# A two-layer decoder on one core: most large products by Strassen's seven products, x spilled between the norms, score operands padded to 128 rows

## The chip, the cores and the metric

One core of a Trainium2 chip runs the whole program. The metric is device time in microseconds (us) of one execution, the median over runs. Engines are named as in the profile: PE (TensorE, the matrix engine), DVE (VectorE), ACT (ScalarE), POOL (GpSimd), SP (SyncE, which here only issues DMAs).

## The reference

The input x is 512 tokens by 1024 features. Each of two layers is a half-step SwiGLU FFN ("A"), a mixing part ("M") and a second FFN ("B"); every part is wrapped in two RMS norms:

```python
for l in range(DEPTH):
    x = x + 0.5 * rms_norm(swiglu(rms_norm(x, g[0]), w_ffn1_in[l], w_ffn1_out[l]), g[1])
    y = mixing_sublayer(rms_norm(x, g[2]), mem, ...)
    x = x + rms_norm(y, g[3])
    x = x + 0.5 * rms_norm(swiglu(rms_norm(x, g[4]), w_ffn2_in[l], w_ffn2_out[l]), g[5])
```

`swiglu` multiplies by 1024 x 5632 weights, forms silu(a) * b (2816 wide), and multiplies back to 1024. The mixing part projects h to z (2048 wide: queries, keys and values), runs three attentions on it (16 heads: 6 of a sliding window with sinks, 6 dilated in three groups, 4 into 256 memory tokens), multiplies three branch projections by sigmoid gates (h times 1024 x 3072 weights), adds them and projects once more (`w_o`). All data are float32.

## The kernel before

All data lie transposed: features on the 128 partitions, tokens along the row, so that x is eight tiles (`X`) of 128 x 512, resident in SBUF throughout. To keep float32 accuracy at the matrix engine's float32r rate, each operand is split into a high part (a rounding copy on ACT) and a low part (the difference, on DVE), and a product is three matmuls, hi\*hi, hi\*lo and lo\*hi (`mm3`, line 348). Weights come as 128 x 1024 blocks of 512 KB: `load` (line 308) issues the DMA on SP into a `raw` tile, ACT writes `wh`, DVE writes `wl` = raw - wh. Five slots each hold raw, wh and wl tiles.

A product of a 128 x 128 weight block and 512 tokens is one matmul of 512 columns (`group`, line 361). Only the first unit of each stage (tiles ab0, z0, and the last four tiles of a stage's output, y_A, y_B, y_wM) goes in two halves of 256 tokens, so that it can begin while the other half's norm is not finished. Per FFN, `ffn` (line 471) runs 11 units of a (two 128-feature tiles), b (two) over k = 8: 96 matmuls of 512 columns each, or 192 of 256 for the first. The output goes in three chunks of 8, 8 and 6 of the 22 middle tiles, with PSUM results added to Y on DVE: 456 matmuls of 512 and 144 of 256. In the mixing part, z takes 192 matmuls of 256 and 288 of 512, the gates 576 of 512.

The norm's scale R is not applied to h: the product runs on x * gain, and DVE multiplies each result by R when it takes it out of PSUM (POOL does so once more for the FFN's b half, behind the silu, line 490) (ab -> s, line 488; z, line 637; gates, line 901). So the matrix engine can begin a stage before R is known. `tail` (line 444) ends each stage: half i's sum of squares, `rstd_cols` (PE column sums, DVE, POOL's power), `rows` (PE spreads the result over the partitions), `post_tile` (x += y * R * gain), `pre_tile` (the next h in two parts), and `pre_stat` for the next R.

In the attentions, `stack_q` (line 709) puts a head's high part on its 64 partitions and its low part on the other 64, `stack_k` (line 720) the high part of the key twice. A score block is then one matmul over 128 rows and one more over 64 rows with the key's low part (`scores`, line 733). Softmax: DVE takes the maximum, ACT the exponentials, POOL divides (`norm_p`), PE transposes, and `pv` (line 762) multiplies by the values, 64 output rows at a time, first all blocks of head g = 0, later all of g = 1. Sigmoids run behind the last exponential (`nc.behind(last_exp)`, line 903).

The order is not the program's. The class `Plan` records all operations with a rank (program order, weights 250 ranks ahead), and `Plan.run` (line 155) replays them with assumed costs: each engine takes, of the operations whose inputs and slots are there, the one of lowest rank. The result is a fixed instruction order for each engine, and semaphores keep the dependences. As all instructions are emitted in one place, every record of the trace has line 250; tiles are told apart by their names.

Of the kernel before, what the change touches and what calls it, by code (L numbers as in the profile page):

```python
# [14 lines left out]
P = 128  # L15
# [5 lines left out]
N_BIG, N_RAW, N_WH, N_WL = 51, 5, 5, 5  # L21
AHEAD = 250
NEG = -1e30
CHUNKS = ((0, 8), (8, 8), (16, 6))
# [7 lines left out]
class Plan:  # L32
    """Records the program in order and emits it as a list schedule: each engine takes, of the operations
    whose operands and tile slots are there, the one of the lowest rank."""
# [10 lines left out]
    class _Pool:  # L45
        def __init__(self, plan, pool, bufs, reserve):
            self.plan, self.pool, self.bufs, self.reserve = plan, pool, bufs, reserve

        def tile(self, shape, dtype, name, tag="t", bufs=None):
            kw = {} if bufs is None else {"bufs": bufs}  # L50
            t = self.pool.tile(shape, dtype, tag=tag, name=name, **kw)
            self.plan.home[t.tensor.name] = (self.pool.name if hasattr(self.pool, "name") else id(self.pool), tag)
            self.plan.slots[self.plan.home[t.tensor.name]] = bufs or self.bufs
            self.plan.reserve[self.plan.home[t.tensor.name]] = self.reserve
            return t

    def __init__(self, tc, ctx):
        self.tc, self.ctx = tc, ctx
        self.ops, self.hist = [], {}
        self.home, self.slots, self.reserve = {}, {}, {}  # L60
        self.rank, self.also = 0, set()
# [3 lines left out]
    def pool(self, name, bufs, space=None, reserve=None):  # L65
        """reserve: slots that only the tile next in rank may take; None: tiles come in rank order."""
        kw = {"space": space} if space is not None else {}
        return Plan._Pool(self, self.ctx.enter_context(self.tc.tile_pool(name=name, bufs=bufs, **kw)), bufs, reserve)
# [8 lines left out]
    @contextmanager  # L77
    def behind(self, ops):
        """What is recorded here also waits for these operations."""
# [51 lines left out]
    def _cost(self, engine, op, outs, ins, k):  # L131
        """The schedule's weights: how long the engine is held, and when the result is there."""
# [6 lines left out]
        if engine == "tensor":  # L139
            n = self._width(outs[0])  # L140
            t = max(n / 2.4, 54) * (4 if op == "matmul" and ins[0].dtype == F32 and n > 1 else 1)
            return t, t + 220
        psum = any(v.space == PSUM for v in outs + ins)
        if engine == "scalar":
            t = 100 + 0.833 * n + 93 * sum(is_ for is_ in (hasattr(k.get("scale"), "ap"), hasattr(k.get("bias"), "ap"),
                                                         k.get("accum_out") is not None))
        elif engine == "vector":
            slow = {"tensor_copy": 1.04 if psum else 0.52, "tensor_scalar": 1.04 if psum else 0.52, "memset": 0.3,
                    "reciprocal": 8.4}
            t = 70 + slow.get(op, 1.04) * n  # L150
        else:
            t = 630 if k.get("op") == ALU.pow else 100 + {"tensor_tensor": 2.2, "tensor_copy": 3.4}.get(op, 0.91) * n
        return t, t + 200

    def run(self):
# [4 lines left out]
        uses, first = {}, {}  # L160
        for i, (_, _, _, _, _, preds, tiles, rank) in enumerate(ops):
# [3 lines left out]
            for t in tiles:  # L165
                uses[t] = uses.get(t, 0) + 1
                first.setdefault(t, (rank, i))
        queue = {}
        for t, r in sorted(first.items(), key=lambda x: x[1]):
            queue.setdefault(self.home[t], []).append(t)  # L170
# [8 lines left out]
        def fits(i):  # L179
# [4 lines left out]
            for h, ts in need.items():  # L184
                if free[h] < len(ts):
                    return False
                front = queue[h][head[h]] in ts
                r = self.reserve[h]
                if not front and (r is None or free[h] - len(ts) < r):
# [6 lines left out]
        while len(order) < n:  # L196
            moved = False
            for e in self.ENGINES:
# [20 lines left out]
                for t in ops[got][6]:  # L219
                    if t not in placed:  # L220
                        placed.add(t)
                        h = self.home[t]
                        free[h] -= 1
                        while head[h] < len(queue[h]) and queue[h][head[h]] in placed:
# [29 lines left out]
def trunk(ctx, tc, xT, memT, rel, gains, mgains, sinks, bgate, w1i, w1o, wz, wkv, wg, wbr, wo, w2i, w2o,  # L254
# [3 lines left out]
    const = pool("const", 1, reserve=0)  # L258
    xpool = pool("xpool", 1, reserve=0)
# [785 lines left out]
```

## Time and profile before

| | |
|---|---|
| median of 3 runs | 2342.35 us (2339.41 to 2342.63) |
| the profiled execution: span of its instructions | 2345.8 us |
| PE busy | 2308.3 us, 98% of the span |
| DVE, ACT, POOL busy | 1070.0, 862.3, 422.1 us (46, 37, 18%) |
| DMA | 216 MB, 92 GB/s on average |

The profiled execution's own time is not listed apart from its span, which lies 3.4 us above the median of the runs. In a timeline row, the first number is the start in us from the span's start, the second the duration; a matmul's recorded duration includes its way through the array, so the pace of a stream of matmuls is read from starts, not from durations.

### The profile page before, as it was taken

Reading aid. Unit: us, or ns where it says so; the run is one execution under the profiler, and the core shown is the slowest. Engines: PE = TensorE matmul, PEld = TensorE weight load, DVE = VectorE, ACT = ScalarE, POOL = GpSimd, SP = SyncE. Lnnn points to the kernel's source line nnn. Section 1 sums busy time; section 2 is a strip of 40 time slices with the busy share of each in tenths; the row PEclk is TensorE's granted clock in tenths of the full one; section 3 lists DMA queues with packets and bytes.
Section 4 is the critical chain, followed back from the end, with each engine's and each line's share of the span. In section 5 each row is a group of like instructions: output and inputs, shape, how many; then the busy total and the mean of one; then the engine's idle time right before and its main releaser. Section 6 shows DMA issues by size and latency. Waiting matters only on the chain. (4 is left out here: it accounts for less than half of the span.)

```text
span 2345.8 us, 29066 instructions
## 1 busy us (share of the span) xinstructions
PE 2308.3 (98%) x11496; PEld 1929.2 (82%) x11496; DVE 1070.0 (46%) x1713; ACT 862.3 (37%) x1477; POOL 422.1 (18%) x450
## 2 busy tenths in 40 slices
PE   8999999999999999999999999999999999999997
PEld 7788889777888888888888888897778889888886
DVE  5424346644544552443473343475445436424343
ACT  5323234554333532322343232255453335332231
POOL 5401013210112320101231100141101214101012
PEclk9999999999999999999999999999999999999998
DMA  6433333112223222332233333321112322323231
GB/s 206 125 99 110 119 99 100 64 37 63 81 90 100 81 100 81 108 102 96 81 99 99 98 110 120 99 89 56 52 39 91 100 80 92 107 91 107 72 108 37
DMA packets 67080, 216.22 MB, mean 92 GB/s; under 512 B 8010, under 2 KB 15231, under 8 KB 66944
## 3 DMA queue, kind: packets, MB, share of 16 engines
q1 hardware_dynamic: 65344, 211.64, 28.1%
q0 software_dynamic: 1600, 2.72, 0.5%
q8 instruction: 90, 1.47, 0.2%
q14 instruction: 46, 0.38, 0.0%
HBM read 210.91 MB, written 3.42 MB: 91 GB/s over the span
## 5 line engine op out<-in xcount | busy, mean ns | idle before, releaser
L250 POOL TENSOR_TENSOR s<-s,R_wM 128x512 f32<-128x512 f32 (+1 forms) x48 | 69.4, 1449 | 534.2 <-ACT s L250 534.2
L250 ACT ACTIVATE s<-s 128x512 f32<-128x512 f32 (+1 forms) x96 | 56.2, 593 | 214.2 <-DVE s L250 214.2
L250 POOL TENSOR_TENSOR s<-s,R_B 128x512 f32<-128x512 f32 (+1 forms) x24 | 32.3, 1350 | 271.7 <-ACT s L250 261.4
L250 POOL TENSOR_TENSOR s<-s,R_s 128x512 f32<-128x512 f32 (+1 forms) x24 | 31.9, 1333 | 242.2 <-ACT s L250 231.8
L250 DVE TENSOR_TENSOR x<-x,upd 128x256 f32<-128x256 f32 x88 | 44.5, 533 | 0.0
L250 POOL TENSOR_TENSOR g02M<-g02M,g00M 128x512 f32<-128x512 f32 x2 | 2.6, 1282 | 209.5 <-issue 209.5
L250 POOL TENSOR_TENSOR sq_A<-sq_A,sq_A 128x256 f32<-128x256 f32 x24 | 19.8, 843 | 49.0 <-ACT sq_A L250 43.0
L250 POOL TENSOR_TENSOR sq_B<-sq_B,sq_B 128x256 f32<-128x256 f32 x24 | 18.3, 783 | 56.1 <-ACT sq_B L250 55.9
L250 DVE TENSOR_TENSOR wl_a4B<-raw_a4B,wh_a4B 128x1024 fp32r<-128x1024 f32 x4 | 4.9, 1226 | 41.3 <-ACT wh_a4B L250 41.3
L250 DVE TENSOR_TENSOR wl_a4A<-raw_a4A,wh_a4A 128x1024 fp32r<-128x1024 f32 x4 | 4.9, 1225 | 41.3 <-ACT wh_a4A L250 41.3
L250 ACT ACTIVATE hh_wM<-x,gt 128x256 fp32r<-128x256 f32 x32 | 15.2, 505 | 21.0 <-DVE x L250 20.9
L250 DVE TENSOR_TENSOR wl_wo1M<-raw_wo1M,wh_wo1M 128x1024 fp32r<-128x1024 f32 x8 | 9.9, 1257 | 27.8 <-ACT wh_wo1M L250 27.6
L250 DVE SCALAR_TENSOR_TENSOR hl_A<-x,gt,hh_A 128x256 fp32r<-128x256 f32 x32 | 21.8, 699 | 0.0
L250 DVE TENSOR_TENSOR wl_o01A<-raw_o01A,wh_o01A 128x1024 fp32r<-128x1024 f32 x8 | 9.8, 1226 | 24.4 <-ACT wh_o01A L250 24.2
L250 DVE TENSOR_TENSOR wl_o01B<-raw_o01B,wh_o01B 128x1024 fp32r<-128x1024 f32 x8 | 9.8, 1225 | 24.4 <-ACT wh_o01B L250 24.1
L250 DVE TENSOR_TENSOR wl_o11B<-raw_o11B,wh_o11B 128x1024 fp32r<-128x1024 f32 x8 | 9.8, 1225 | 24.4 <-ACT wh_o11B L250 24.1
L250 DVE TENSOR_TENSOR wl_o11A<-raw_o11A,wh_o11A 128x1024 fp32r<-128x1024 f32 x8 | 9.8, 1225 | 23.2 <-ACT wh_o11A L250 22.9
L250 PE MATMUL ab0B<-hh_wM,wl_b0B 128*128 128x256 f32 x64 | 18.3, 286 | 1.7 <-DVE wl_b0B L250 1.7
L250 ACT ACTIVATE hh_A<-x,gt 128x256 fp32r<-128x256 f32 x32 | 15.2, 504 | 12.4 <-DVE x L250 12.3
L250 ACT CAST wh_a8A<-raw_a8A 128x1024 fp32r<-128x1024 f32 x4 | 4.2, 1054 | 41.9 <-PE y11A L250 33.2
L250 ACT CAST wh_a8B<-raw_a8B 128x1024 fp32r<-128x1024 f32 x4 | 4.2, 1054 | 41.9 <-PE y11B L250 33.2
L250 POOL TENSOR_TENSOR sq_q0A<-sq_q0A,sq_q0A 128x256 f32<-128x256 f32 x14 | 17.3, 1236 | 11.7 <-ACT sq_q0A L250 8.1
(2804 smaller groups left out, 8158.9 us busy)
## 6 DMA issues: line engine op xcount, KB each, us to landing
raw_o00A<-in_w1o SPq DMA_DIRECT2D x8, 512.0 KB, 3.4
raw_o01A<-in_w1o SPq DMA_DIRECT2D x8, 512.0 KB, 3.4
raw_o10A<-in_w1o SPq DMA_DIRECT2D x8, 512.0 KB, 3.4
raw_o11A<-in_w1o SPq DMA_DIRECT2D x8, 512.0 KB, 3.5
raw_wo0M<-in_wo SPq DMA_DIRECT2D x8, 512.0 KB, 3.9
raw_wo1M<-in_wo SPq DMA_DIRECT2D x8, 512.0 KB, 3.9
raw_o00B<-in_w2o SPq DMA_DIRECT2D x8, 512.0 KB, 3.3
raw_o01B<-in_w2o SPq DMA_DIRECT2D x8, 512.0 KB, 3.4
```

The source lines that it names most:

```text
L250: getattr(getattr(self.tc.nc, e), op)(*a, **k)
```

## The change

- **Seven products.** The product of weights in 2 x 2 blocks (two output tiles i by two halves of the features j) and activations in 2 x 2 blocks (halves of the features, halves of the tokens) is formed with seven block products instead of eight, in Strassen's form by Winograd: four sums of weight blocks (s1 to s4, POOL), four of activation blocks (t1 to t4, POOL), and seven additions of results (ACT copies, DVE). Each of the seven weight operands is split into high and low parts. All matmuls have 256 columns. It is used for units 2 to 10 of each FFN's input product (`gated`, `quarters`), all of the output product (`out_chunk`, `out_last`, chunks of 2, 3, 3 and 3 of the 11 pairs of middle tiles), the gates (six blocks of `quarters`), and units 2 and 3 of four of z. Units 0 and 1 of the FFN and of z stay direct, in halves of 256 tokens (`direct`, 192 matmuls of 256 each).
- **Norms.** h is now multiplied by R before it is split (`Hs.half`), because t1 to t4 add tokens of different R. So R of a half must be known before the first matmul on that half, and `next_h` runs: update of x, sum of squares, R, h, for one half and then the other. The results no longer need a multiplication by R.
- **x spilled.** x is written to DRAM by SP when h is formed (`spill`, four DMAs of 256 KB a half) and read back before the next update (`load_x`); there are 63 big tiles in place of 51.
- **Attention.** The key's low part is padded with zeros to 128 rows, so both score matmuls have 128 rows. `pv` takes the heads g = 0 and 1 of each block in turn. The factor 1/8 of the queries moves into `stack_q`.
- **Others.** The memory's keys and values are computed inside `next_h`, between the two halves, before the mixing part. The bias tables' 39 DMAs go to SP's queue instead of POOL's. The sigmoid of a block's first quarter reads PSUM directly. `Plan` has new cost figures and another rule for slots; weights have 7 raw, 4 wh and 4 wl slots.

The core of the diff:

```diff
-N_BIG, N_RAW, N_WH, N_WL = 51, 5, 5, 5
-AHEAD = 250
+N_BIG, N_RAW, N_WH, N_WL = 63, 7, 4, 4
...
-CHUNKS = ((0, 8), (8, 8), (16, 6))
+CHUNKS = ((0, 2), (2, 3), (5, 3), (8, 3))
...
+    def parts2(r, n, nm):
+        h = whp.tile([P, 1024], F32R, tag="wh", name="wh_" + nm)
+        lo = wlp.tile([P, 1024], F32R, tag="wl", name="wl_" + nm)
+        nc.scalar.copy(h[:, :n], r[:, :n])
+        nc.vector.tensor_tensor(lo[:, :n], r[:, :n], h[:, :n].bitcast(F32), op=ALU.subtract)
+        return h, lo
...
+        def sum(self, a, b, op, nm):
+            n = self.c * 256
+            s = raw.tile([P, 1024], F32, tag="raw", name=f"{nm}_{self.nm}")
+            nc.gpsimd.tensor_tensor(s[:, :n], a[:, :n], b[:, :n], op=op)
+            return s
...
+        b11, b12, b21, b22 = u0[:, :HF], u0[:, HF:], u1[:, :HF], u1[:, HF:]
+        ta = big.tile([P, S], F32, tag="b", name="ta_" + nm)
+        tb = big.tile([P, S], F32, tag="b", name="tb_" + nm)
+        t1, t3, t2, t4 = ta[:, :HF], ta[:, HF:], tb[:, :HF], tb[:, HF:]
+        nc.gpsimd.tensor_tensor(t1, b12, b11, op=ALU.subtract)
+        nc.gpsimd.tensor_tensor(t2, b22, t1, op=ALU.subtract)
+        nc.gpsimd.tensor_tensor(t3, b22, b12, op=ALU.subtract)
+        nc.gpsimd.tensor_tensor(t4, b21, t2, op=ALU.subtract)
...
+            two(u0[:, :HF], ["b11"], HF)
+            two(u1, ["b21", "b22"], S)
+        two(ta, ["t1", "t3"], S)
+        two(tb, ["t2", "t4"], S)
+        return f
...
+    def product(bk, w, pairs, key, first):
+        for p, f in enumerate(pairs):
+            for b in range(2):
+                dst = bk[:, b * HF:(b + 1) * HF]
+                wh, wl = at(w, p, b)
+                xh, xl = f[key]
+                end = p == len(pairs) - 1 and b == 1
+                nc.tensor.matmul(dst, wh, xh, start=first and p == 0 and b == 0, stop=False, skip_group_check=not first)
+                nc.tensor.matmul(dst, wh, xl, start=False, stop=False, skip_group_check=not first)
+                nc.tensor.matmul(dst, wl, xh, start=False, stop=end, skip_group_check=not first)
...
+        with nc.ahead(-AHEAD):
+            a11 = blk.raw(0, 0)
+            w1 = blk.parts(a11, "a11")
+            s3 = blk.sum(a11, blk.raw(1, 0), ALU.subtract, "s3")
+            w7 = blk.parts(s3, "s3")
+            s1 = blk.sum(blk.raw(1, 0), blk.raw(1, 1), ALU.add, "s1")
+            w5 = blk.parts(s1, "s1")
+            s2 = blk.sum(s1, a11, ALU.subtract, "s2")
+            w6 = blk.parts(s2, "s2")
+            w2 = blk.parts(blk.raw(0, 1), "a12")
+            w4 = blk.parts(blk.raw(1, 1), "a22")
+            s4 = blk.sum(blk.raw(0, 1), s2, ALU.subtract, "s4")
+            w3 = blk.parts(s4, "s4")
+        A, D = bank(mmp, "A" + nm), bank(mmp, "D" + nm)
+        C, B = bank(mmp, "C" + nm), bank(mmp, "B" + nm)
+        e = big.tile([P, S], F32, tag="b", name="e" + nm)
+        fg = big.tile([P, S], F32, tag="b", name="fg" + nm)
+        product(A, w1, pairs, "b11", True)
+        nc.scalar.copy(e, A)
+        product(D, w7, pairs, "t3", True)
+        nc.scalar.copy(fg, D)
+        product(C, w5, pairs, "t1", True)
+        nc.vector.tensor_tensor(fg, fg, C, op=ALU.add)
+        product(B, w6, pairs, "t2", True)
+        nc.vector.tensor_tensor(e, e, B, op=ALU.add)
+        product(A, w2, pairs, "b21", False)
+        c11(A)
+        others(1, 1, fg, e)
+        product(D, w4, pairs, "t4", False)
+        others(1, 0, e, D)
+        product(C, w3, pairs, "b22", False)
+        others(0, 1, e, C)
...
+    def spill(half, nm):
+        for m in range(4):
+            t = dram.tile([P, S], F32, tag=f"xs{half}{m}{nm}", name=f"xs{half}{m}{nm}")
+            nc.sync.dma_start(t, X[half][m])
+            spilled[half][m] = (t, False)
...
+        def half(self, half, R, l, n):
+            for m in range(4):
+                key = m // 2, half, m % 2
+                nm = f"{m}{half}{self.nm}"
+                u = self.u[key] = big.tile([P, S], F32, tag="b", name="hn" + nm)
+                hi = self.hi[key] = big.tile([P, S], F32R, tag="b", name="hh" + nm)
+                lo = self.lo[key] = big.tile([P, S], F32R, tag="b", name="hl" + nm)
+                for b in range(2):
+                    c = slice(b * HF, b * HF + HF)
+                    f = m // 2 * 4 + 2 * b + m % 2
+                    nc.vector.scalar_tensor_tensor(u[:, c], X[half][m][:, c], gcol(l, n, f), R[:, :HF], op0=ALU.mult, op1=ALU.mult)
+                nc.scalar.copy(hi, u)
+                nc.vector.tensor_tensor(lo, u, hi.bitcast(F32), op=ALU.subtract)
...
+    def next_h(l, n, nm, update, blk, first=None, filler=None):
+        h = Hs(nm)
+        for half in range(2):
+            if update is not None:
+                update(half)
+            h.half(half, stat(X[half], f"q{half}{nm}", op), l, n)
+            if update is not None:
+                spill(half, nm)
+            if half == 0:
+                if filler is not None:
+                    h.extra = filler()
+                h.w = (first or direct_weights)(blk)
+        h.finish()
...
+            def others(i, half, x, y):
+                t = x if (i, half) == (1, 1) else big.tile([P, S], F32, tag="b", name="c")
+                nc.vector.tensor_tensor(t, x, y, op=ALU.add)
+                nc.scalar.activation(t[:, :HF], t[:, :HF], AF.Silu)
+                nc.vector.tensor_tensor(u[i][:, HALVES[half]], t[:, :HF], t[:, HF:], op=ALU.mult)
+            quarters(blk, h.pairs, f"{g}{nm}", c11, others)
+            return u
...
+        def out_chunk(ci, pairs):
+            c0, cn = CHUNKS[ci]
+            first = ci == 0
+            for s in range(2):
+                blk = Block(wout[l, s], c0, cn, f"o{ci}{s}{nm}")
+                with nc.ahead(-AHEAD):
+                    w = weights(blk, ("a11", "s3", "s1", "s2", "a12", "a22", "s4"), {})
+                A, D, C, B = (bank(mmp, f"{x}{ci}{s}{nm}") for x in "ADCB")
+                product(A, w["a11"], pairs, "b11", True)
+                take(s, "E", A, first)
+                product(D, w["s3"], pairs, "t3", True)
+                take(s, "F", D, first)
...
+                product(C, w["s4"], pairs, "b22", False)
+                take(s, "C", C, first)
...
-            nc.gpsimd.dma_start(vec[h0:h0 + nh, :n], v[:nh, :n])
+            nc.sync.dma_start(vec[h0:h0 + nh, :n], v[:nh, :n])
...
+                lo = t[:, n:] if 2 * n <= S else big.tile([P, S], F32R, tag="b", name=f"kl{g}{name}")
+                nc.vector.memset(lo[b, :n].bitcast(F32), 0.0)
                 nc.vector.tensor_tensor(lo[a, :n], z[a], t[a, :n].bitcast(F32), op=ALU.subtract)
...
         def scores(dst, qs, ks, g, qcols, kcols):
-            a, _ = parts(g)
             hi, lo = ks
             nc.tensor.matmul(dst, qs[g][:, qcols], hi[g][:, kcols], start=True, stop=False)
-            nc.tensor.matmul(dst, qs[g][a, qcols], lo[a, kcols], start=False, stop=True)
+            nc.tensor.matmul(dst, qs[g][:, qcols], lo[g][:, kcols], start=False, stop=True)
...
                 for j, kb in enumerate(ks):
-                    lhs = V[:, kb * P + vcol:kb * P + vcol + 64] if kind != "mem" else V[:, kb, vcol:vcol + 64]
-                    nc.tensor.matmul(o[64 * g:64 * g + 64, cols(b)], lhs, T[i], start=(j == 0),
-                                     stop=(j == len(ks) - 1))
+                    for g in range(2):
+                        c = vcols[g]
+                        lhs = V[:, kb * P + c:kb * P + c + 64] if kind != "mem" else V[:, kb, c:c + 64]
+                        nc.tensor.matmul(o[64 * g:64 * g + 64, cols(b)], lhs, Ts[g][i], start=(j == 0),
+                                         stop=(j == len(ks) - 1))
...
+            def c11(A):
+                for b in range(2):
+                    sigmoid(b, 0, tile_of(b, 0)[:, :HF], A[:, b * HF:(b + 1) * HF])
```

In `out_last` the products that make the first half of the tokens come first for both halves of the output features, and the two products with s1 and s4, which only the second half needs, come last. The second half of `w_o` runs its two halves of the tokens one after the other in the same way, 96 matmuls of 256 each.

## Rows read from the trace of the kernel before

**Rows 1.** The page: busy time of each engine, granted clock in 40 slices

```profile
PE 2308.3 (98%) x11496; PEld 1929.2 (82%) x11496; DVE 1070.0 (46%) x1713; ACT 862.3 (37%) x1477; POOL 422.1 (18%) x450
...
PEclk9999999999999999999999999999999999999998
```

**Rows 2.** Busy time by stretch (us, engine busy (x count), clock, DMA): seams, start, end

```profile
0.00:40.00 40.00, 30.54 (x215) 28.95 (x216) 24.96 (x43) 26.74 (x59) 24.24 (x35) 1.00 0.78 250
370.00:430.00 60.00, 56.91 (x466) 55.91 (x465) 45.81 (x88) 32.36 (x69) 28.25 (x30) 1.00 0.27 89
760.00:835.00 75.00, 72.44 (x511) 67.10 (x510) 41.31 (x73) 38.56 (x79) 31.48 (x33) 1.00 0.27 85
1150.00:1210.00 60.00, 57.36 (x422) 54.12 (x422) 45.20 (x85) 29.86 (x66) 30.31 (x35) 1.00 0.25 80
...
2315.00:2346.00 31.00, 17.20 (x134) 16.65 (x132) 13.92 (x35) 2.92 (x7) 13.27 (x18) 0.78 0.20 69
```

**Rows 3.** Timeline of PE: first and last of 28 successive 512-wide products

```profile
299.74 0.39 PE L250 MATMUL ab8A<-hh_s,wl_b8A 128*128 128x512 f32 x1
...
305.86 0.39 PE L250 MATMUL ab8A<-hh_s,wl_b8A 128*128 128x512 f32 x1
```

**Rows 4.** Timeline of PE: first and last of 30 successive 256-wide products

```profile
32.01 0.28 PE L250 MATMUL ab0A<-hh_s,wh_b0A 128*128 128x256 f32 x1
...
35.48 0.28 PE L250 MATMUL ab0A<-hh_s,wl_a0A 128*128 128x256 f32 x1
```

**Rows 5.** Timeline of PE: score matmuls of 256, then of 128 columns

```profile
432.51 0.38 PE L250 MATMUL s0m00M<-k0c0M,q0c0M 128*128 128x256 f32 x1
432.82 0.38 PE L250 MATMUL s0m00M<-klc0M,q0c0M 64*128 64x256 f32 x1
...
558.26 0.32 PE L250 MATMUL sob10M<-klb1M,q0b1M 64*128 64x128 f32 x1
558.51 0.33 PE L250 MATMUL sob10M<-k0b1M,q0b1M 128*128 128x128 f32 x1
```

**Rows 6.** Timeline of PE: probabilities times values, and the product behind

```profile
509.20 1.09 PE L250 MATMUL oa1M<-pta11M,VvaM 128*64 128x128 f32 x8
510.22 0.50 PE L250 MATMUL z4M<-hh_A,wl_z4M 128*128 128x512 f32 x1
```

**Rows 7.** Timelines of DVE and POOL: both busy at once, or one alone

```profile
169.15 1.23 DVE L250 TENSOR_TENSOR wl_b5A<-raw_b5A,wh_b5A 128x1024 fp32r<-128x1024 f32 x1 [0.21 <-ACT wh_b5A L250]
...
169.73 1.80 POOL L250 TENSOR_TENSOR s<-s,R_s 128x512 f32<-128x512 f32 x1 [4.18 <-ACT s L250]
...
622.90 1.29 POOL L250 TENSOR_TENSOR g02M<-g02M,g01M 128x512 f32<-128x512 f32 x1 [0.76 <-DVE g01M L250]
...
29.52 0.74 POOL L250 TENSOR_TENSOR sq_s<-sq_s,sq_s 128x256 f32<-128x256 f32 x1
30.91 4.11 POOL L250 TENSOR_TENSOR sq_s<-sq_s,sq_s 128x256 f32<-128x256 f32 x3
...
30.93 1.81 DVE L250 TENSOR_TENSOR wl_a1A<-raw_a1A,wh_a1A 128x1024 fp32r<-128x1024 f32 x1 [1.50 <-ACT wh_a1A L250]
```

**Rows 8.** Timelines around one norm: sum, root, row, update

```profile
380.00 0.50 PE L250 MATMUL st_p0A<-ones,sq_A 128*128 128x1 f32 x4
...
382.64 0.48 DVE L250 SCALAR_TENSOR_TENSOR upd<-y0A,gt,row_p0A 128x256 f32<-128x256 f32 x1 [1.45 <-PE row_p0A L250]
383.04 0.47 DVE L250 SCALAR_TENSOR_TENSOR upd<-y1A,gt,row_p0A 128x256 f32<-128x256 f32 x1
383.43 0.41 DVE L250 TENSOR_TENSOR y5A<-y5A,y_A 128x256 f32<-128x256 f32 x1
...
386.16 2.00 ACT L250 CAST wh_vc<-raw_vc 128x1024 fp32r<-128x1024 f32 x2 [0.42 <-ACT sq_q0A L250]
```

**Rows 9.** Busy time from the last z product to the last Exp; that Exp

```profile
550.00:598.00 48.00, 48.00 (x239) 36.11 (x238) 18.88 (x92) 24.19 (x72) 0.00 (x0) 0.93 0.14 45
...
597.32 0.22 ACT L250 ACTIVATE wgtM<-wgtM 128x24 f32<-128x24 f32 x1 [2.76 <-DVE wgtM L250]
```

More of the change, by code (lines that the diff above doesn't have):

```diff
@@ L166, in run @@
                 uses[t] = uses.get(t, 0) + 1
-                first.setdefault(t, (rank, i))
-        queue = {}
+                first[t] = min(first.get(t, (rank, i)), (rank, i))
+                last[t] = max(last.get(t, (rank, i)), (rank, i))
+        queue, place = {}, {}
         for t, r in sorted(first.items(), key=lambda x: x[1]):
-            queue.setdefault(self.home[t], []).append(t)
+            q = queue.setdefault(self.home[t], [])
+            place[t] = len(q)
+            q.append(t)
+        left = {}
+        for h, q in queue.items():
+            live, room = [], []
+            for t in q:
+                while live and live[0] < first[t]:
+                    heapq.heappop(live)
+                heapq.heappush(live, last[t])
+                room.append(self.slots[h] - len(live))
+            if min(room) < 0 and not self.turns[h]:
+                raise RuntimeError(f"{h}: {-min(room)} slots short, first at {next(t for t, r in zip(q, room) if r < 0)}")
+            left[h] = room
         head = {h: 0 for h in queue}
@@ L186, in fits @@
                     return False
-                front = queue[h][head[h]] in ts
-                r = self.reserve[h]
-                if not front and (r is None or free[h] - len(ts) < r):
+                far = max(place[t] for t in ts)
+                if far - head[h] >= len(ts) and self.turns[h]:
+                    return False
+                if far - head[h] >= len(ts) and min(left[h][head[h]:far], default=len(ts)) < len(ts):
                     return False
@@ L223, in run @@
                         free[h] -= 1
+                        for at in range(head[h], place[t]):
+                            left[h][at] -= 1
                         while head[h] < len(queue[h]) and queue[h][head[h]] in placed:
@@ new lines, in direct @@
+    def direct(h, w, nm, evict):
+        for t, tok in enumerate(HALVES):
+            banks = [bank(mmp, f"{nm}{t}{b}") for b in range(2)]
+            for k in range(KD):
+                for b in range(2):
+                    for i in range(2):
+                        wh, wl = at(w[i, k // 4], k % 4, b)
+                        xh, xl = h.parts(k, t)
+                        dst = banks[b][:, i * HF:(i + 1) * HF]
+                        nc.tensor.matmul(dst, wh, xh, start=k == 0 and i == 0, stop=False)
+                        nc.tensor.matmul(dst, wh, xl, start=False, stop=False)
+                        nc.tensor.matmul(dst, wl, xh, start=False, stop=k == KD - 1 and i == 1)
+            evict(t, banks)
@@ L647, in z_group, with z_at @@
[L647 to L653 removed]
+        def z_at(nme, half):
+            rate = {"qb1": 4, "kb1": 4, "vb1": 4, "qb2": 16, "kb2": 16, "vb2": 16}.get(nme, 1)
+            if nme not in Z:
+                Z[nme] = big.tile([P, S], F32, tag="b", name=f"{nme}{nm}")
+            if rate == 1:
+                return Z[nme][:, HALVES[half]], lambda v: v
+            n = HF // rate
+            return (Z[nme].rearrange("p (r i) -> p r i", r=rate)[:, :, half * n:(half + 1) * n],
+                    lambda v: v.rearrange("p (i r) -> p r i", r=rate))
```

649 lines of the change are left out of this document (382 added, 267 removed).

## The prediction

> **What bounds the kernel now.** I read the page first: PE is busy 98% of the span, and its clock is full but for the end [rows 1]. Such a share says only that something is always in the array, so the pace comes from starts in PE's timeline: 28 products of 512 columns start 6.12 us apart from first to last, 0.2267 us each [rows 3]; 30 of 256 columns 3.47 us, 0.1197 us each [rows 4]. A 256-column product costs 53% of a 512-column one, so each cut in two adds 0.0127 us. Next the busy time by stretch: where one part hands over to the next, PE idles 3.1, 2.6 and 2.6 us (60 less 56.91, 75 less 72.44, 60 less 57.36); the start costs 9.5 and the end 13.8 us [rows 2]. So the kernel is bound by the number of matmul columns, and the sum starts there. DVE (46%) and POOL (18%) look free, but the change loads both.
>
> **Matmuls removed.** Per FFN, before: 240.7 us in (192 x 0.1197 + 960 x 0.2267) and 120.6 us out (456 x 0.2267 + 144 x 0.1197), together 361.3 [rows 3, 4]. After, at the same pace: two direct units of 192 and nine units of 7 x 24 = 168, and an output of 11 x 84 = 924, all of 256: 46.0 + 181.0 + 110.6 = 337.6 us. An eighth of the columns goes, but half of that is given back, since all products are of 256. Four FFNs: -95 us if PE stays the bound. Gates: 576 x 0.2267 = 130.6 us become 1008 x 0.1197 = 120.7 per layer, -20 us in all. z: 88.3 become 86.2, -4 us. The Trainium skill (TensorE: Matmul & The Clock Gate, Wait — 56ns, not 53.3ns?) puts the fixed cost of a product at about 2.5 ns beyond columns over 2.4 GHz; the rows give 13, five times that. By the page the cut in two would cost almost nothing, and the removal would come to about 60 us more; the rows decide.
>
> **What feeds the matmuls.** One unit of seven products lasts 168 x 0.1197 = 20.1 us on PE. For it DVE must do work with two operands in SBUF: seven wl of 1024 elements (1.23 us [rows 7]), four of 512 (0.68, between 0.41 at 256 and 1.23 at 1024 [rows 7, 8]) and four of 256 (0.41): 13.0 us; successive instructions overlap by 0.08 us (0.48 long, 0.40 apart [rows 8]), so 11.8 us. POOL adds four weight sums of 1024 (0.74 at 256 and 1.29 at 512 give 2.4 [rows 7]) and four of 256: 12.5 us. Alone, each fits in 20.1 us. Together they don't: while DVE's wl_b5A ran (169.15 to 170.38), POOL's 512-wide product took 1.80 instead of 1.29 us, ending 1.15 us behind DVE's end; and wl_a1A, begun with POOL at work, took 1.81 instead of 1.23 [rows 7]. They take turns. So a unit needs about 24.3 us of the shared path against 20.1 on PE and 21.8 before (96 x 0.2267). An output block of three pairs needs DVE 6.2 and POOL 7.4 us, 13.6 of PE's 126 x 0.1197 = 15.1 (its additions read PSUM, and I count them free of this). A chunk of three units and two output blocks: 72.9 + 27.2 = 100.1 us in turns, 90.5 on PE. A handover to POOL saves 0.14 us (1.29 less 1.15), one back to DVE as much, of which 0.08 is counted; if they alternate at all of POOL's 32 instructions, 100.1 comes down to about 94. I take the middle, 97. The first chunk (two direct units, two pairs: 46.0 + 20.1 us) stays PE's. An FFN is then 66.1 + 3 x 97 = 357 us, -4, and -15 us for four, where PE alone would give -95. Bounds: 90.5 a chunk (-95), and 117 if DVE's PSUM work (2.8 us a unit, 8.6 in two output blocks) never runs beside POOL's (+220). Gates need 18 to 19 us in turns of PE's 20.1, with the merges' additions between: I take -15 of the -20.
>
> **Scores.** Score matmuls alternate between 128 and 64 rows, and start 0.31 us apart at 256 columns, 0.25 at 128 [rows 5], where same-shape products take 0.12 [rows 4]: a switch of row shape costs 0.19. Per layer 80 of 256 and 48 of 128: two layers 160 x 0.31 + 96 x 0.25 = 74 us; without the switch 160 x 0.12 + 96 x 0.06 = 25. I take -48.
>
> **Values.** The 208 products of probabilities and values run as two records of 0.109 us each, 45 us (8 records in 0.87 us and an exit of 0.2 [rows 6]). In turns between the two column halves they may overlap (-22) or pay that exit, some 0.09, each time (+19). The nearest row is the same-shape stream itself, which gives 0, and half as many entries and exits; I take -10.
>
> **Attention's stalls.** From the last z product to the last Exp, 48 us, PE was 100% busy, but it filled the time with gates [rows 9]. Now a gate block's first quarter stays in its bank until that Exp, so PE has one block (20 us) and most of a second as filler, and its own attention work shrinks by 12 to 17 us. If the chain of DVE and ACT keeps its 48 us, PE lacks 0 to 15 us a layer. POOL's sums also queue ahead of `norm_p`. I take +8 a layer, +16.
>
> **Seams.** h now waits for R. From a half's last result: addition 0.7, square 0.6, addition 0.7, and from st to the update 2.64 [rows 8]; update of four tiles 4 x (2 x 0.40 + 0.6) = 5.6; square and sum 1.5; R again 2.64; the first tile of h two multiplications, an ACT copy and a difference, 2.2: some 17 to 18 us to the first matmul. Under it PE has 72 products (8.6 us) behind an FFN and 96 (11.5) behind `w_o`; before the mixing part also the memory's 96 (11.5). The second half's chain shares DVE with the first's, and ends some 2 us behind the 11.5 us of matmuls of the first. So PE idles 8.5 us at M to B (twice) and 11 at B to A (once), 2 at A to M (twice), and after the long gaps its clock falls once each, 3.4 us (48 us at 0.93 [rows 9]). Against [rows 2] that is +9 (two times), +12 and -1 (two times). At the start, the first matmul waits for x, R and h, to about 17 us where it was 7, partly won back in the streams: +6. The end's chain is about 2 us shorter. Sum +32; bounds +10 and +70. The cover here is short: anything late in this chain is late on PE.
>
> **SP.** Each half's four spills and loads of x (256 KB) and the 39 table DMAs stand in SP's one queue, and a spill that waits for DVE's x holds the weight loads behind it. Weights are loaded four products ahead, which hides it; if not, one or two landings are exposed, 0 to +7. I take +2. Landings themselves have room at the share of [rows 2].
>
> **Sum.** FFN -15, gates -15, z -4, scores -48, values -10, attention +16, seams +32, SP +2: -42 us. The profiled execution's span is 2345.8, 3.4 above the median of 2342.35, so the sum is taken off the median: **2300 us**.
>
> **Rivals.** *PE stays the bound*: DVE and POOL overlap enough that a chunk costs 90.5. For it: outside the overlaps [rows 7], DVE's and POOL's instructions keep their length, and PE's slack in the output blocks could absorb them. Against: a unit's sum of turns is 4 us above PE's time. It gives -95 for the FFNs: 2300 - 80 = 2220 us. Chance 0.23. *The shared path decides the FFNs*: sums on POOL lie at the head of the chain of weights (s1, s2, s4), each holds DVE for 2.4 us, and DVE's queue is in order, so PSUM work waits behind blocked differences. Without the FFNs the sum is -27, so the kernel is slower when an FFN costs over 7 us more than before, a chunk over 100.6; at 105 it gives 2342 - 27 + 4 x 19.8 = 2394 us. Chance 0.22. The Trainium skill (SBUF — State Buffer, Who interferes with whom) states it as a rule: a DVE instruction with two SBUF inputs and a GpSimd instruction that reads SBUF exclude each other for the whole of the first one's run. The trace agrees, with 1.80 against 1.29 us. *Padding does nothing*: the 0.19 us of a score matmul is not the switch of rows; then 2300 + 48 = 2348. Chance 0.03, as no row of equal shapes shows such a gap. The forecast keeps 0.52; its own range, from a chunk of 94 to 100 and the bounds of values and stalls, is 2255 to 2345.
>
> **How the numbers follow.** A measurement of this kernel tells some 0.2%, 5 us, from no change. The forecast is faster in nine tenths of its 0.52, the first rival always: 0.47 + 0.23, and a little of the others: faster 0.72. Slower: the second rival's 0.22 and the forecast's tail, 0.23. Same: 0.05. The range 2210 to 2395 leaves out half of the first rival's lower and half of the second's upper side.
>
> **What would show it.** Starts of same-shape products 0.12 us apart; score matmuls at 0.12 and 0.06; in a unit (tiles named as the banks A, D, C, B of a unit), PE idle for wl or for POOL's sums, some 3 us, and POOL's 1024-wide sums well over 2.4 us where DVE is busy; gaps of 8 to 11 us at three seams, with the clock down behind them. Units at 20 us on PE with no idle time would show the first rival; units over 27 us the second. The forecast is wrong if the seams' gaps exceed 20 us each, or the time in the attentions grows.

## The result, and the profile after

The changed kernel takes 2550.44 us (median of 4 runs, 2549.1 to 2557.37), the kernel before 2342.12: a ratio of 1.0892, 95% interval 1.0872 to 1.0913. The forecast was 2300 us, and its range ended at 2395. Sign and range were wrong. Some names first: a *chunk* is one of four parts of an FFN (units of the input product, then output blocks over their results); d0 and d1 are an FFN's two direct units, with which its first chunk begins; a *seam* is the stretch where one stage hands over to the next, M to B from the mixing part to the second FFN.

The page of the changed kernel (all its records carry line 279) answers to [rows 1]: busy times, clock, and two of its groups with their mean ns.

```profile
PE 2265.8 (89%) x17208; PEld 2175.5 (85%) x17208; DVE 2106.8 (83%) x2501; ACT 1198.1 (47%) x1989; POOL 1335.3 (52%) x775
...
PEclk9999999899999899999989999998999998999998
...
L279 POOL TENSOR_TENSOR s_i7A<-raw_i7A,raw_i7A 128x1024 f32<-128x1024 f32 x4 | 14.5, 3615 | 15.0 <-DMA raw_i7A<-in_w1i 7.6
...
L279 DVE TENSOR_TENSOR wl_s_i8A<-s_i8A,wh_s_i8A 128x1024 fp32r<-128x1024 f32 x8 | 19.5, 2440 | 0.0
```

PE has lost its 98%. DVE's busy time doubled, only in part by work: a difference of 1024 elements takes 2.44 us on average in one unit where [rows 7] have 1.23 alone, and POOL's sum 3.6 where 2.4 was forecast. I call **excess** the time of DVE's records above the 10th percentile of the same operation and shape: it is 615 us, before 63. So of the 1037 us that DVE's busy time rose by, 552 are excess.

The busy time by stretch of the second FFN of layer 0 shows where it goes (columns as in [rows 2]): its first chunk, the three others, then the seams M to B and B to A.

```profile
863.50:944.50 81.00, 73.84 (x565) 71.53 (x566) 62.26 (x77) 38.22 (x61) 43.28 (x29) 0.95 0.16 51
944.50:1050.80 106.30, 95.00 (x758) 92.98 (x757) 101.44 (x86) 46.25 (x67) 68.91 (x34) 0.97 0.30 94
1050.80:1157.00 106.20, 96.03 (x759) 94.26 (x758) 96.33 (x91) 45.62 (x65) 63.47 (x32) 0.97 0.36 110
1157.00:1272.00 115.00, 101.19 (x770) 98.65 (x768) 101.17 (x100) 49.61 (x73) 71.35 (x38) 0.94 0.33 104
...
840.00:865.00 25.00, 16.69 (x107) 15.65 (x106) 19.62 (x32) 10.06 (x15) 7.89 (x7) 0.78 0.27 94
1255.00:1290.00 35.00, 23.20 (x133) 21.28 (x132) 29.76 (x49) 14.14 (x21) 15.06 (x11) 0.72 0.42 146
```

A chunk takes 106 us where 97 was forecast, the last one 115, the first 81 where 66 was, and in a chunk DVE is busy for 96 to 101 of 106 us. Around the seams the mean granted clock is 0.78 and 0.72: behind the gap at M to B the products of d0 start 0.21 us apart up to 867.8 us, at 1.2 GHz, and 0.12 from there on, at 2.4.

Inside a chunk, timelines of DVE (first six rows) and POOL (last three), start and duration in us:

```profile
1059.25 2.86 DVE L279 TENSOR_TENSOR wl_a_i5B<-raw_i5B,wh_a_i5B 128x1024 fp32r<-128x1024 f32 x1 [0.49 <-ACT wh_a_i5B L279]
1062.03 0.67 DVE L279 TENSOR_TENSOR fg5B<-fg5B,C5B 128x512 f32<-128x512 f32 x1
1062.62 2.82 DVE L279 TENSOR_TENSOR wl_s_i5B<-s_i5B,wh_s_i5B 128x1024 fp32r<-128x1024 f32 x1
1065.37 0.68 DVE L279 TENSOR_TENSOR e5B<-e5B,B5B 128x512 f32<-128x512 f32 x1
1066.08 2.19 DVE L279 TENSOR_TENSOR fg5B<-fg5B,e5B 128x512 f32<-128x512 f32 x1
1068.19 3.43 DVE L279 TENSOR_TENSOR wl_a_i6B<-raw_i6B,wh_a_i6B 128x1024 fp32r<-128x1024 f32 x1
...
1057.87 3.15 POOL L279 TENSOR_TENSOR s_i6B<-raw_i6B,raw_i6B 128x1024 f32<-128x1024 f32 x1 [6.53 <-DMA raw_i6B<-in_w2i]
1061.28 3.08 POOL L279 TENSOR_TENSOR s_i6B<-raw_i6B,raw_i6B 128x1024 f32<-128x1024 f32 x1 [0.26 <-DMA raw_i6B<-in_w2i]
1064.44 3.28 POOL L279 TENSOR_TENSOR s_i6B<-s_i6B,raw_i6B 128x1024 f32<-128x1024 f32 x1
```

Each difference that meets a sum ends 1.1 us, nearly its own 1.23, behind the end of that sum: 1061.02 and 1062.11, 1064.36 and 1065.44. The additions with one operand in PSUM (C5B, B5B) keep 0.67 us while POOL's sum runs. The addition behind them (fg5B with e5B, both in SBUF) takes 2.19. So DVE's instructions with both operands in SBUF and POOL's sums go in turns here, and the work with an operand in PSUM is free of it.

From the first matmul to the last of each stage, worked out from PE's starts, and what is left between stages, start and end included (us; labels are those of the experiments below):

| | FFNs (4) | mixing (2) | between | span |
|---|---|---|---|---|
| before | 1486.3 | 816.6 | 42.9 | 2345.8 |
| after | 1642.9 | 791.0 | 113.4 | 2547.3 |
| e2_no_sums | 1447.7 | 740.8 | 110.5 | 2298.9 |
| e7_sums_aside | 1649.2 | 798.1 | 109.9 | 2557.2 |
| e8_fill_aside | 1454.5 | 736.9 | 109.8 | 2301.1 |
| e1_sums_dve | 1552.3 | 742.4 | 114.0 | 2408.7 |
| e6_no_sums_no_R | 1463.8 | 755.6 | 67.2 | 2286.6 |
| e9_q_first | 1663.2 | 801.9 | 100.7 | 2565.8 |
| e3_before_scores_pv | 1489.4 | 745.1 | 41.8 | 2276.4 |

After less before: FFNs +156.6, mixing -25.6, between +70.5, together the 201.5 us of the spans. The time between stages isn't all idle: at A to M, PE makes the memory's products there, 72 of a layer's 96 before and 91 after, so 19 x 0.12 = 2.3 us a layer of the +70.5 have only moved.

### The profile page after: what moved, and what is told of

Read it like the earlier page. It is cut to its first block, busy times and chain, and to the rows that moved or that the text cites. A ratio compares the mean times of both kernels' runs of the same rounds, so it can differ in the third digit from the quotient of the medians.

```text
span 2547.3 us, 43150 instructions
## 1 busy us (share of the span) xinstructions
PE 2265.8 (89%) x17208; PEld 2175.5 (85%) x17208; DVE 2106.8 (83%) x2501; ACT 1198.1 (47%) x1989; POOL 1335.3 (52%) x775
## 5 line engine op out<-in xcount | busy, mean ns | idle before, releaser
L279 ACT ACTIVATE c<-c 128x256 f32<-128x256 f32 x72 | 30.1, 417 | 67.6 <-DVE c L279 67.6
L279 DVE TENSOR_TENSOR x<-x,upd 128x512 f32<-128x512 f32 x48 | 41.8, 871 | 0.2
L279 DVE TENSOR_TENSOR wl_s_g3M<-s_g3M,wh_s_g3M 128x1024 fp32r<-128x1024 f32 x8 | 20.5, 2568 | 2.8 <-ACT wh_s_g3M L279 2.8
L279 POOL TENSOR_TENSOR s_i7A<-raw_i7A,raw_i7A 128x1024 f32<-128x1024 f32 x4 | 14.5, 3615 | 15.0 <-DMA raw_i7A<-in_w1i 7.6
L279 POOL TENSOR_TENSOR s_i4B<-raw_i4B,raw_i4B 128x1024 f32<-128x1024 f32 x4 | 14.2, 3554 | 13.4 <-DMA raw_i4B<-in_w2i 13.4
L279 POOL TENSOR_TENSOR s_i10B<-raw_i10B,raw_i10B 128x1024 f32<-128x1024 f32 x4 | 14.3, 3565 | 13.2 <-DMA raw_i10B<-in_w2i 13.2
L279 POOL TENSOR_TENSOR s_o10A<-raw_o10A,raw_o10A 128x768 f32<-128x768 f32 x4 | 14.1, 3536 | 13.2 <-DMA raw_o10A<-in_w1o 13.2
L279 POOL TENSOR_TENSOR s_i10A<-raw_i10A,raw_i10A 128x1024 f32<-128x1024 f32 x4 | 14.5, 3616 | 11.5 <-DMA raw_i10A<-in_w1i 11.5
L279 DVE TENSOR_TENSOR wl_s_i8A<-s_i8A,wh_s_i8A 128x1024 fp32r<-128x1024 f32 x8 | 19.5, 2440 | 0.0
L279 POOL TENSOR_TENSOR s_i6B<-raw_i6B,raw_i6B 128x1024 f32<-128x1024 f32 x4 | 11.9, 2984 | 14.4 <-DVE wl_a_i5B L279 7.6
L279 DVE TENSOR_TENSOR wl_s_i8B<-s_i8B,wh_s_i8B 128x1024 fp32r<-128x1024 f32 x8 | 19.4, 2425 | 0.0
```

Of the source, the lines that this page charges most:

```text
L279: getattr(getattr(self.tc.nc, e), op)(*a, **k)
```

## The experiments

**Is it POOL's sums? Leave them out, or make them on DVE.**

```diff
         def sum(self, a, b, op, nm):
...
-            nc.gpsimd.tensor_tensor(s[:, :n], a[:, :n], b[:, :n], op=op)
-            return s
+            return a
```

> The kernel after, with the weight sums left out (the sum returns its first operand; the output is then not the product that Strassen's scheme needs), all differences, casts and matmuls kept. T1: POOL's share of the exclusion goes, a chunk takes 91 to 97 us, the kernel 2300 to 2400 us, and DVE's busy time falls by over 400 us although none of its instructions is removed. T2: DVE's count is unchanged, so a chunk stays above 103 us and the kernel above 2500 us. T3 (the pace is set by PE, whose clock falls after each short gap): as T2 as long as the gaps stay.

```diff
         def sum(self, a, b, op, nm):
...
-            nc.gpsimd.tensor_tensor(s[:, :n], a[:, :n], b[:, :n], op=op)
+            nc.vector.tensor_tensor(s[:, :n], a[:, :n], b[:, :n], op=op)
...
-        nc.gpsimd.tensor_tensor(t1, b12, b11, op=ALU.subtract)
+        nc.vector.tensor_tensor(t1, b12, b11, op=ALU.subtract)
...
```

and so for t2 to t4, here and where they are made from h.

> The kernel after, with every weight sum (s1 to s4) and every combination t1 to t4 made on DVE instead of POOL; nothing else changes. Theory T1 (DVE instructions with two SBUF operands and POOL's SBUF work shut each other out, and POOL's 1024-wide sums hold the pair for 2.4 us each): the same sums cost 1.2 us on DVE, a unit then asks 20 to 21 us of DVE alone, so a chunk falls from 106 to 92 to 98 us and the kernel takes 2330 to 2450 us; the excess of DVE's instructions over their uncontended length falls from 615 to under 150 us. Rival T2 (DVE is simply overloaded with 2107 us of its own work): DVE gets some 280 us more, the kernel takes over 2600 us.

Measured: 2300.06 us without the weight sums (the sums t1 to t4 of activation blocks stay on POOL; ratio to before 0.9808, 0.9764 to 0.9852), 2413.24 with weight and activation sums on DVE (1.0297, 1.026 to 1.0334). One chunk by stretch, without the sums, then with them on DVE:

```profile
959.60:1050.80 91.20, 91.03 (x759) 90.83 (x758) 71.14 (x89) 46.95 (x65) 13.13 (x12) 1.00 0.41 128
```

```profile
996.10:1094.20 98.10, 92.71 (x759) 91.20 (x758) 90.79 (x121) 46.27 (x65) 0.00 (x0) 1.00 0.38 119
```

Both came out as T1 had it, the chunk with sums on DVE at the top of its 92 to 98 us, and DVE's own work (T2) is refuted. T3 isn't told apart by these two, since the gaps in a chunk went with the sums; a clock of 0.97, which two of the changed kernel's chunks have, is worth 3 us of their 106. Without the sums PE is busy for 91.03 of a chunk's 91.20 us, and DVE's busy time falls from 2106.8 to 1685.7 us with the same 2501 instructions. With the sums on DVE the chunk is 8 us shorter although DVE has 91 instructions without an operand in PSUM where it had 60, and its excess falls to 62 us. Without the weight sums it is still 160: the 100 us between are left with the activation sums on POOL, which go to DVE here. PE is now busy for 92.71 and DVE for 90.79 of 98.10 us; most of PE's waits end at a DVE result, but that DVE alone sets this pace isn't shown.

**Do late sums delay the weights, or do the sums shut DVE out?** POOL makes every weight sum, but nobody reads it (e7); or POOL only fills (e8). In both, the tile `dump` takes the place of one of the seven raw slots.

```diff
-N_BIG, N_RAW, N_WH, N_WL = 63, 7, 4, 4
+N_BIG, N_RAW, N_WH, N_WL = 63, 6, 4, 4
...
-            nc.gpsimd.tensor_tensor(s[:, :n], a[:, :n], b[:, :n], op=op)
-            return s
+            nc.gpsimd.tensor_tensor(dump[:, :n], a[:, :n], b[:, :n], op=op)
+            return a
```

> The changed kernel, where POOL still makes every weight sum, but into a tile that nobody reads; the weights are taken from the first operand (the output is then not Strassen's). Nothing waits for POOL's sums any more, except the load that reuses the raw tile. T1 (exclusion): DVE's excess stays over 350 us and the kernel at 2430 to 2560 us. Rival T1b (what costs is that weights wait for late sums at the head of their chain): excess under 200 us as without sums, 2295 to 2345 us.

```diff
-N_BIG, N_RAW, N_WH, N_WL = 63, 7, 4, 4
+N_BIG, N_RAW, N_WH, N_WL = 63, 6, 4, 4
...
-            nc.gpsimd.tensor_tensor(s[:, :n], a[:, :n], b[:, :n], op=op)
-            return s
+            nc.gpsimd.memset(dump[:, :n], 0.0)
+            nc.gpsimd.memset(dump[:, :n], 0.0)
+            return a
```

> As the run before it, but each sum on POOL is replaced by two fills of the same width with a constant (POOL writes, but reads nothing). If only POOL's reading of SBUF shuts DVE out: DVE's excess under 200 us and 2295 to 2330 us. If any POOL instruction on SBUF does: over 2350 us, by the fills' length.

Measured: 2562.02 us with the sums put aside (1.0919, 1.0857 to 1.0981), 2301.11 with fills (0.9807, 0.9755 to 0.9858). Two chunks with sums that nobody reads:

```profile
947.60:1056.60 109.00, 97.24 (x759) 94.71 (x758) 102.84 (x88) 46.47 (x67) 70.17 (x34) 0.95 0.28 91
1056.60:1162.00 105.40, 96.41 (x758) 94.58 (x757) 99.02 (x89) 45.94 (x65) 63.83 (x32) 0.95 0.34 111
```

With fills, a chunk by stretch:

```profile
865.00:956.00 91.00, 90.92 (x758) 90.72 (x757) 70.08 (x88) 47.37 (x67) 61.38 (x70) 1.00 0.33 107
```

and timelines of POOL and of DVE in it:

```profile
867.46 12.95 POOL L279 MEMSET dump<- 128x768 f32 x16
...
869.03 1.23 DVE L279 TENSOR_TENSOR wl_a_i2B<-raw_i2B,wh_a_i2B 128x1024 fp32r<-128x1024 f32 x1 [1.65 <-ACT wh_a_i2B L279]
871.91 1.23 DVE L279 TENSOR_TENSOR wl_a_i2B<-raw_i2B,wh_a_i2B 128x1024 fp32r<-128x1024 f32 x1 [1.66 <-ACT wh_a_i2B L279]
```

This settles it. That nobody waits for a sum any more (T1b) gains nothing; what costs is that POOL reads SBUF for a sum, which a fill doesn't: DVE's excess is 657 us with unread sums, 170 with fills (160 without either). POOL was busy with fills for 573 us in the first 950, 48 us of the chunk above (the rest of its 61.38 are sums of activations), and DVE's differences of 1024 elements kept a median of 1.23 us; with unread sums their median is 2.84. The fills wait for no load, so POOL made all 672 of them by 940 us, and only that part of the run tests them. It suffices: the first FFN takes 371 us with fills, 369 without either, 421 with unread sums; the first mixing part 367, 371 and 399.

**What opens the seams? h without the wait for R.**

```diff
+    one = const.tile([P, HF], F32, tag="one", name="one")
+    nc.vector.memset(one, 1.0)
...
         def half(self, half, R, l, n):
+            R = one
```

> The kernel without the weight sums, and h made with ones in place of the row R of rstd (the second norm is left out of the result; its squares, its root and its row are still computed, but nothing waits for them). Theory S1 (the new wait of h for R is what opens the seams): square, sum, root and row are a leg of 4.5 to 6 us, so the gaps ahead of d0 and z0 shrink from 12 to 14 us to 6 to 9, the first matmul comes at 11 to 13 us instead of 17.5, and the kernel falls from 2300 to 2255 to 2275 us, clock falls included. Rival S2 (the leg from the last result to the updated x, and the four tiles' differences, set the gaps): 2285 to 2300 us.

> The same single edit (ones in place of R in h) in the changed kernel, with its sums on POOL. S1: 2550 falls to 2500 to 2530 us. S2: 2535 to 2550 us. In both the chunks of three units stay at 104 to 108 us, since no norm lies inside them.

Measured: 2289.88 us without the sums (0.9759, 0.9708 to 0.981), 2531.43 with them (1.0788, 1.0735 to 1.0842): 10 and 19 us gained. The time between stages falls by 43 and by 46 us (to 67.7 in the second), as much as S1 asked for at most (45 us for the whole kernel), but FFNs and mixing take back 31 and 27. One seam, M to B from the w_o products to the second direct unit, without the sums: first with the wait, then without.

```profile
770.00:821.30 51.30, 41.46 (x283) 39.81 (x282) 42.31 (x64) 24.96 (x38) 22.81 (x16) 0.83 0.19 67
```

```profile
770.00:815.20 45.20, 39.05 (x281) 37.94 (x280) 43.54 (x62) 23.58 (x37) 24.32 (x16) 0.89 0.22 76
```

The first matmul of d0 comes 2.4 us behind the last w_o product instead of 13.4, and then PE waits inside the unit: DVE is busy for 43.54 of the 45.20 us. The leg through R is worth 6 us of such a seam. The time without the sums lies in S2's range, but not by S2's mechanism, since this gap did close and the wait came back inside the unit; with the sums the gain lies between the two theories' ranges.

DVE's busy time there isn't all work either. Timelines of DVE (first two rows) and POOL in the same stretch of e6:

```profile
809.04 1.78 DVE L279 TENSOR_TENSOR hl31wM<-hn31wM,hh31wM 128x512 fp32r<-128x512 f32 x1
810.75 1.77 DVE L279 TENSOR_TENSOR flt30wM<-t30wM,fht30wM 128x512 fp32r<-128x512 f32 x1
...
808.53 1.75 POOL L279 TENSOR_TENSOR t40wM<-hn20wM,t20wM 128x512 f32<-128x512 f32 x1
810.24 1.73 POOL L279 TENSOR_TENSOR t21wM<-hn31wM,t11wM 128x512 f32<-128x512 f32 x1
```

A difference of 512 elements, 0.68 us alone, takes 1.78 beside POOL's sums of activation blocks, which every kernel here but e1 and the two without Strassen's products (e3, e4) leaves on POOL. The durations of DVE's records in the stretch add up to 48 us, their uncontended durations to 35. So some 13 us of this seam are excess, and each of the 13 records that are stretched by over 0.3 us overlaps a POOL record: the turns again.

**Or the order on PE?** A timeline of PE at a seam of the changed kernel, then four rows of DVE (q0 is the first half's sum for the coming norm, p1 the second half's for the norm of the stage's output; sq are the squares, st their column sums):

```profile
854.67 1.84 PE L279 MATMUL st_p1M<-ones,sqp1M 128*128 128x1 f32 x8 [5.45 <-DVE sqp1M L279]
856.77 1.87 PE L279 MATMUL st_q0wM<-ones,sqq0wM 128*128 128x1 f32 x8 [0.25 <-DVE var_p1M L279]
859.65 1.22 PE L279 MATMUL row_q0wM<-cs,rstd_q0wM 128*128 128x128 f32 x4
863.48 0.80 PE L279 MATMUL d0B<-hh00wM,wh_a_i0B 128*128 128x256 f32 x2 [2.60 <-ACT hh00wM L279]
...
848.77 2.29 DVE L279 TENSOR_TENSOR wl_a_i0B<-raw_i0B,wh_a_i0B 128x1024 fp32r<-128x1024 f32 x1
850.98 0.68 DVE L279 TENSOR_TENSOR sqq0wM<-sqq0wM,sqq0wM 128x512 f32<-128x512 f32 x1
851.58 2.34 DVE L279 TENSOR_TENSOR wl_a_i0B<-raw_i0B,wh_a_i0B 128x1024 fp32r<-128x1024 f32 x2
853.85 0.68 DVE L279 TENSOR_TENSOR sqp1M<-sqp1M,sqp1M 128x512 f32<-128x512 f32 x1
```

The first half's squares (sqq0wM) are summed at 851.66, but st_q0 starts at 856.77: on PE it stands behind st_p1, whose squares come at 854.53 because DVE does the weights' differences ahead of them. So I put the second half's sum behind the first half's norm:

```diff
-            rs.append(stat(Y[half], f"p{half}{nm}", scp))
+            rs.append((lambda half=half: stat(Y[half], f"p{half}{nm}", scp)) if half else stat(Y[half], f"p{half}{nm}", scp))
...
+        row = lambda half: rs[half]() if half else rs[half]
```

> The changed kernel with one change of order at the seams: the second half's post-norm sum (st_p1) is recorded behind the first half's second norm (st_q0), its root and its h, where PE had it ahead of them. Theory S3 (at a seam st_q0 was ready but stood in PE's queue behind st_p1, which waited for the last result): the first matmul of d0 and z0 comes 3 to 6 us sooner at four of five seams, and since the clock falls less long the kernel gains 12 to 30 us: 2520 to 2538 us. Rival S2 (the second half's own chain, now later, holds PE inside d0 and z0 instead): the gap moves into the unit, 2543 to 2555 us.

Measured: 2571.62 us (1.0965, 1.0941 to 1.0989), slower than both theories said. The order was the one wanted, in timelines of PE and DVE at the same seam:

```profile
856.20 1.02 PE L279 MATMUL st_q0wM<-ones,sqq0wM 128*128 128x1 f32 x8 [2.58 <-DVE sqq0wM L279]
859.17 1.22 PE L279 MATMUL row_q0wM<-cs,rstd_q0wM 128*128 128x128 f32 x4 [1.95 <-POOL rstd_q0wM L279]
860.18 1.71 PE L279 MATMUL st_p1M<-ones,sqp1M 128*128 128x1 f32 x8
...
867.12 0.15 DVE L279 TENSOR_SCALAR var_p1M<-st_p1M 128x2 f32<-128x2 f32 x1
871.09 0.87 DVE L279 SCALAR_TENSOR_TENSOR upd<-ym10M,gt,row_p1M 128x256 f32<-128x256 f32 x2 [3.82 <-PE row_p1M L279]
```

The M to B gaps fall from 14.4 to 8.6 us, the other gaps by less than 1, and FFNs and mixing take 20 and 11 us more: from d0's first matmul to that of d1 it is 38.9 us instead of 30.3, because the second half's variance (var_p1M) now stands behind the first half's h on DVE, and its update, which began at 859.74, begins at 871.09. S3 falls. Neither one wait nor one order makes the seam. What both runs leave is the load of DVE's queue there, its own work and its turns with POOL; no run took work off DVE at a seam, so that this is the cause is argued, not shown.

**The attention parts alone, on the kernel before.** Padded scores (e4), and with them the value products in turns (e3):

```diff
+                    nc.vector.memset(lo[b, :n].bitcast(F32), 0.0)
...
-            nc.tensor.matmul(dst, qs[g][a, qcols], lo[a, kcols], start=False, stop=True)
+            nc.tensor.matmul(dst, qs[g][:, qcols], lo[g][:, kcols], start=False, stop=True)
...
+                    for g in range(2):     # in pv, inside the blocks (e3 only)
```

> The kernel before with only the padded scores: 2295 to 2310 us if the switch of row shape costs what the records say; 2335 to 2345 us if the time then waits elsewhere. The difference to the kernel with both attention parts is the worth of the value products in turns, 10 to 22 us.

> The kernel before, with the attention parts of the change alone: K padded to 128 rows in the scores, and the two heads' probability-value products in turns. From the changed kernel's records: score matmuls 0.12 us apart at either width (before 0.31 and 0.25), so -43 us, and the value products 32 us less 52 in a layer's count, -20 us: 2270 to 2295 us if PE's time is the time of the kernel there. Rival (the attention waits for DVE and ACT behind the faster products): 2310 to 2340 us.

Measured: 2295.9 us (0.9791, 0.9763 to 0.9819) and 2275.02 us (0.9705, 0.9676 to 0.9733). The page of e3:

```profile
PE 2236.8 (98%) x11496; PEld 1891.5 (83%) x11496; DVE 1077.9 (47%) x1737; ACT 861.0 (38%) x1477; POOL 423.2 (19%) x450
...
PEclk9999999999999999999999999999999999999998
```

and its score matmuls of 128 columns in PE's timeline:

```profile
535.83 0.28 PE L250 MATMUL sob10M<-k0b1M,q0b1M 128*128 128x128 f32 x1
535.94 0.28 PE L250 MATMUL sob10M<-kl0b1M,q0b1M 128*128 128x128 f32 x1
536.05 0.27 PE L250 MATMUL sob10M<-k0b1M,q0b1M 128*128 128x128 f32 x1
```

Scores now start 0.11 us apart where [rows 5] show 0.25. The products with the values, in the changed kernel's timeline of PE:

```profile
621.10 0.27 PE L279 MATMUL ob0M<-ptb01M,Vvb0M 128*64 128x128 f32 x1
621.11 0.27 PE L279 MATMUL ob0M<-ptb00M,Vvb0M 128*64 128x128 f32 x1
621.21 0.27 PE L279 MATMUL ob0M<-ptb01M,Vvb0M 128*64 128x128 f32 x1
621.22 0.27 PE L279 MATMUL ob0M<-ptb00M,Vvb0M 128*64 128x128 f32 x1
```

The two heads, in different column halves, start 0.01 us apart, a pair every 0.11 us where [rows 6] have 0.109 for each single one. The scores are worth 48 us (2344.37, the median of before beside these runs, less 2295.9), the values 21, and all of it arrives while PE stays 98% busy. e3 beats both kernels. It also beats the changed kernel with its weight sums for nothing (2300): in this form Strassen's products would not pay even then.

## Why the prediction was wrong, step by step

**What bounds the kernel before; the pace of matmuls.** Right. Without the sums a chunk takes 91.2 us, 90.5 by [rows 4]. Of some 243 us between the forecast's -42 and the spans' +201.5, the FFNs make 172 (+156.6 against -15); the mixing part and the time between stages make the rest.

**What feeds the matmuls: this step failed.** The mechanism was named, and its price was too low. I had 100.1 us for a chunk in turns, and took 97 because [rows 7] show handovers that save 0.14 us. The runs show no such saving over a chunk: adding up the records of two of them at their uncontended durations gives DVE's instructions with SBUF operands only 52 and 53 us and POOL 54 and 50, 106 and 103 together, and the chunks took 106.3 and 106.2. The PSUM work (17 and 19 us) runs beside it, as I had counted. This FFN then has 9 us more than forecast in each of two chunks, 18 in the last, and 15 in the first. (Four times 357 less 361.3 is also -17, not the -15 that I wrote.) The exclusion's worth over the whole kernel is the changed kernel less the one without sums: 195 us in the FFNs, 50 in the mixing part; with unread sums less without, it is 202 and 57. The Trainium skill (SBUF — State Buffer, Who interferes with whom) names this lock between two SBUF inputs on DVE and a GpSimd instruction that reads SBUF, and exempts one that only writes. The unread sums (2562 us, the first FFN 421) and the fills (the first FFN 371) agree with both halves.

**The first chunk "stays PE's", and the seams, +32: the second failure.** Even without the weight sums it takes 78.8 us (d0 at 789.7, A2 at 868.5), not 66.1, of which d0 has 31.6 where PE alone needs 23.0; and the time between stages is 68 us above that of before. The rival in which PE stays the bound was priced at 2220 us. Its condition nearly holds without the sums (a chunk takes 91.2 us, not 90.5), and that kernel takes 2300. I counted a seam as a chain of latencies mainly over one half (its terms add up to 16.6 us, not 17 to 18). It is a stretch in which DVE has both halves' updates, h in two parts and the weights' differences, in order, with PE's matmuls in a fixed order too: in e6, 35 us of DVE's own work and 13 of turns with POOL (its records overlap a little) for the 45 us from the w_o products to the second unit. I had put these turns at nothing in the seams. The clock was the smaller part: the 0.21 us between products lasts 4.3 us into d0, some 2 us lost. ([rows 9], from which I took 3.4 us a gap, show a fall while PE had no gap.) Of the 70.5 us between stages some 66 remain when the moved products are taken off, against +32 and a bound of +70; what the seams do inside the units behind them came on top. How much of a seam is DVE's work, the turns and the order stays open.

**Scores -48, values -10.** Right, and too small for the values: 48 and 21. The 48 has some luck in it: I took 0.06 us for a product of 128 columns, and the rows of e3 have 0.11, by which the sum is 44. The Trainium skill (TensorEngine Tiling (Array Packing), Key Properties) has different column tiles work independently; the two products 0.01 us apart agree.

**Gates -15, z -4, stalls +16.** Without sums the mixing part takes 740.8 us, with the attention parts alone 745.1, so these three seem worth -4 together, -3 by the forecast. That agreement is partly luck. In the first, 24 of the memory's products a layer have left the mixing part, 5.8 us in all, so the three come to some +1. And the stalls were not what I had: from the last z product to the last Exp, PE idles 2.3 and 1.5 us in the two layers without the weight sums (before 0.0), where I had 8 each. Gates and z were not tried by themselves. With the sums on POOL the mixing part takes another 50 us; I had given the gates 18 to 19 us in turns and a loss of 5 in all.

**SP, +2.** Nothing in the runs speaks against it; it was not tried by itself.

**The rivals and the range.** The one that came true, with 0.22, was priced by a chunk of 105 us and my own seams, 2394. Of its two mechanisms the turns held; that the sums lie at the head of the weights' chain did not matter (e7). Its sign, units over 27 us, did not show either: in the FFN above, units took 20 to 25 us, and the first output block of its two middle chunks 24 where PE alone needs 15. My upper bound for a chunk, 117, stood in the text and not in the range.

## What to carry to other kernels

Before moving work to an idle engine, ask whether it shares a path to memory with the one that is already needed: two engines at 46% and 18% were one resource here for what DVE reads from SBUF twice and POOL reads at all, so these uncontended durations have to be added, in full. A busy share can hide it: part of DVE's busy time was waiting. Saved matrix columns must pay for their sums, splits and additions on the vector engine. And when you cost a handover between stages, add up the whole load of its busiest queue, both halves and the turns with other engines, beside the latency of one chain.

## What was not expected of the hardware

POOL's fills cost nothing in the 940 us that hold them (first FFN and mixing part 738 us with them, 740 without), while sums that no one uses cost 80 us there and some 260 in the whole kernel. Two 64-column products with different column halves start 0.01 us apart and together take the 0.11 us of one. And around the gap of 14 us at M to B the granted clock was half from 854.1 to 867.8 us, but only the last 4.3 us of that lie under products of the next unit, so the gap itself cost far more than the clock.
